# A two-layer streaming trunk on one core: the normalised input built in four-chunk steps on VectorE, and 10 instead of 16 chunks on the unnormalised one

## The chip, the cores and the metric

The kernel runs on one core of a Trainium2 chip. The metric is the device time of one execution in microseconds (us). Engines are named as the profile names them: PE is TensorE's matmuls (PEld its weight loads), DVE is VectorE, ACT is ScalarE, POOL is GpSimd, SP is SyncE, which only issues DMAs here.

## What is computed

A trunk of two layers runs over 304 tokens that share their weights: 16 meta tokens, 256 frames of a new stream and 32 frames of a running one. Activations are kept transposed, channels on the partitions: 1024 channels are eight blocks of 128 x 304. Cut to what matters:

```
def trunk_layer(h, ...):
    h = layer_norm(ALPHA * h + 0.5 * swiglu(h, up1, down1), ln_g[0], ln_b[0])
    q_r, k_r, v_r, g_r, q_s, k_s, v_s, u, gates = split(h @ w_in)
    ...  # retention, stick-breaking attention, pooling, gated merge
    h = layer_norm(ALPHA * h + mix, ln_g[1], ln_b[1])
    h = layer_norm(ALPHA * h + 0.5 * swiglu(h, up2, down2), ln_g[2], ln_b[2])
```

A layer norm takes, for each token, the mean and the variance over all 1024 channels, subtracts, scales, and then applies a gain g and a bias b for each channel. What follows a norm is always a large product: the first feed-forward up-projection, `w_in`, or the second up-projection.

## The kernel before

**Products.** Each product is cut into chunks of 128 output channels. A chunk takes eight weight tiles of 128 x 128, and three matmuls for each tile, since weights and activations are held as a high and a low part (hi x hi, hi x lo, lo x hi): 24 matmuls of 304 columns into one PSUM buffer. Most chunks use a ring of three PSUM buffers (`pd`); a few use a ring of five (`pa`). ACT makes the high part of a weight block (`whi`, `prep_hi`, L234) four chunks ahead, DVE the low part (`wlo`, `prep_lo`, L240) three chunks ahead: one 128 x 1024 instruction on each engine for each chunk. Weights stream from HBM on SP's queue.

**Order.** The order on every engine is the order in which the Python code records instructions; each engine works through its own queue in that order. `dense` (L343) records one chunk. It first lets generators in `side` go one step (`pump`), then runs what was deferred (`tick`), then records the chunk's matmuls with the weight preparation, and lastly lets pending epilogues go one step (`advance`).

**The norm and the unnormalised input.** `Norm` (L429) keeps PE working while the statistics of a norm are still being made. Before the statistics are known, the centred input times the gain, `un` (a high and a low part, `unh` and `unl`), is there. The first `UCHUNKS` = 16 chunks behind a norm multiply this unnormalised input, with two more columns (306 instead of 304) that give for each output channel the product with g and with b. Their results are mended afterwards by `value` (L556): for each such chunk DVE copies the two columns out (`cc`, L559), DVE adds the mean's part (`un<-lnn,cc,pd`, L204), which frees the PSUM buffer, and POOL multiplies by the reciprocal standard deviation (`un<-un,rs_y`). Chunks 0 to 2 are led (their k-parts interleaved) and fill the three `pd` buffers, chunks 3 to 5 use `pa`, chunk 6 takes chunk 0's `pd` buffer again, chunk 9 that of chunk 6, chunk 10 that of chunk 7. From chunk 16 on a chunk multiplies the normalised input `hn` (`hnh`, `hnl`) and has no mending.

`run` (L504) is the norm's own generator. It makes the statistics (`stats`), refines the reciprocal root on DVE (`newton`, which ends with `rs_y<-rs_y,rs_t`), and then, one step for each chunk recorded, makes one of the eight channel blocks of `hn`: POOL adds the negative mean and multiplies (`scale`, L528: `x<-x,lnn`, `x<-x,rs_y`), ACT applies gain and bias (`x<-x,vec`) and makes the high part (`hnh<-x`), DVE the low part (`hnl<-x,hnh`).

**Where it stands.** Five norms work in this way. Three are followed by a feed-forward block (spans begin at about 683, 912 and 1570 us in the profile). There a pair of chunks is a gate and an up half: ACT takes the sigmoid (`sg<-un,cc`), DVE multiplies twice (`sg<-un,cc,sg`, in that order) and makes the low part (`sl<-sg,sh`) of what ACT rounds (`sh<-sg`). For normalised chunks the two multiplications read PSUM (`sg<-sg,pd`) and the low part is POOL's. Two norms are followed by `w_in` (at about 243 and 1143 us). Its first 24 chunks are, twice over, four keys (`ks`), four values (`vs`) and four queries (`qs`), which ACT copies out of `un`. After every second value chunk `v_transposes` (L669) records four PE transposes of the finished `vs`; the first four stand in PE's queue right ahead of chunk 8 and read the values of chunks 4 and 5.

Of the kernel before, what the change touches and what calls it, by code (L numbers as in the profile page):

```python
# [10 lines left out]
F32 = mybir.dt.float32  # L11
F32R = mybir.dt.float32r
AF = mybir.ActivationFunctionType
ALU = mybir.AluOpType

D = 1024
KD = 8
# [6 lines left out]
T = MP + SMP  # L24
# [8 lines left out]
EPS_S = EPS / (ALPHA * ALPHA)  # L33
SCALE = 128.0 ** -0.5
TW = T + 2
UCHUNKS = 16
TPD = 8
NRAW = 5
AHEAD = 3
# [128 lines left out]
def trunk(ctx, tc, xT, wts, kc_d, vc_d, s0_d, sp_d, vec_d, tab_d, y_d, kv_d, ret_d, pool_d):  # L168
# [10 lines left out]
    V, A, G, PE, SP = nc.vector, nc.scalar, nc.gpsimd, nc.tensor, nc.sync  # L179
# [7 lines left out]
    def pair_r(name):  # L187
        return ([newquad(f"{name}h{i}", F32R) for i in range(2)],
                [newquad(f"{name}l{i}", F32R) for i in range(2)])
# [10 lines left out]
    def tt(e, out, a, b, op):  # L200
        e.tensor_tensor(out=out, in0=a, in1=b, op=op)  # L201
# [4 lines left out]
    def act(out, in_, f=AF.Copy, **kw):  # L206
        A.activation(out, in_, f, **kw)  # L207
# [135 lines left out]
    def dense(xs, c0, c1=T, pool=None, nside=2):  # L343
        pump(nside)
        tick()
        ps = pa() if pool == "a" else psd.tile([128, 512], F32, tag="d", name="pd")
        n = len(xs)
        o = ps[:, c0:c1]
        for k, (xh, xl) in enumerate(xs):
            wh, wl = wtile()  # L350
            PE.matmul(o, wh, xh[:, c0:c1], start=(k == 0), stop=False)  # L351
            PE.matmul(o, wh, xl[:, c0:c1], start=False, stop=False)  # L352
            PE.matmul(o, wl, xh[:, c0:c1], start=False, stop=(k == n - 1))  # L353
        advance()
        return ps
# [22 lines left out]
    def hl_list(hl, n):  # L378
        return [(hl[0][k // 4][:, k % 4], hl[1][k // 4][:, k % 4]) for k in range(n)]
# [33 lines left out]
    def split_t(x):  # L413
        n = x.shape[-1]
        hi, lo = t304("st_hi", F32R)[:, 0:n], t304("st_lo", F32R)[:, 0:n]
        split(hi, lo, x)
        return hi, lo


    def mean(i, parts, c):  # L420
        p = pa()
        PE.matmul(p[:, c], onesr[:, i], parts[0], start=True, stop=False)
        PE.matmul(p[:, c], onesr[:, i], parts[1], start=False, stop=True)
        return p
# [4 lines left out]
    class Norm:  # L429
# [19 lines left out]
        def chunk(self, n, ps, scale):  # L449
            c, r = self.c, self.r(n)  # L450
            stt(V, r, ps[:, c], scale, r, ALU.mult, ALU.add)
            if n == 1:
                self.s0 = t304("ln0", F32R)
                tt(G, self.s0[:, c], self.r(0), r, ALU.add)
            elif n == 2:
                p = pa()
                PE.matmul(p[:, c], onesr[:, 0], self.s0[:, c], start=True, stop=True)
                self.piv = t304("lnp")
                act(self.piv[:, c], p[:, c])
            elif n == 3:  # L460
                for i in range(4, KD):
                    tt(G, self.r(i), self.r(i), self.piv[:, c], ALU.subtract)
            for i in {3: (0, 1), 4: (2, 3, 4)}.get(n, (n,) if n > 4 else ()):
                start(self.centre(i))
# [39 lines left out]
        def run(self):  # L504
            c = self.c
            parts = [split_t(x[:, c]) for x in (self.s, self.q)]
            yield
            self.stats(*[mean(1, p, c) for p in parts])
            yield
            self.newton()  # L510
            self.ready = True
            self.hl = pair_r("hn")
            yield
            yield
            for n in range(KD + 2):
                if n < KD:
                    self.scale(n)
                if 1 <= n <= KD:
                    r, gb = self.r(n - 1), self.gb[:, n - 1]
                    act(r, r, AF.Identity, scale=gb[:, 0:1], bias=gb[:, 1:2])  # L520
                    act(self.hl[0][(n - 1) // 4][:, (n - 1) % 4, self.c], r)
                if n >= 2:
                    i, j = (n - 2) // 4, (n - 2) % 4
                    hi, lo = self.hl[0][i][:, j, self.c], self.hl[1][i][:, j, self.c]
                    tt(V, lo, self.r(n - 2), hi.bitcast(F32), ALU.subtract)
                yield

        def scale(self, n):  # L528
            r = self.r(n)
            tt(G, r, r, self.nm[:, self.c], ALU.add)  # L530
            tt(G, r, r, self.rs[:, self.c], ALU.mult)

        def finish(self):
            c = self.c
# [35 lines left out]
        def dense(self, c0, epi):  # L570
            i = self.used
            self.used += 1
            if i >= UCHUNKS:
                ps = dense(hl_list(self.hl, KD), c0)
# [11 lines left out]
            self.pending.append((ps, c0, epi))  # L586
            if i == UCHUNKS - 1:
                while self.gen in side:
                    pump(1)
            k = 0  # L590
            while self.ready and self.pending and (k < 2 or i == UCHUNKS - 1):
                p, o, e = self.pending.pop(0)
# [433 lines left out]
    with tc.manual_schedule():  # L1026
# [10 lines left out]
        for l in range(DEPTH):  # L1037
            last = l == DEPTH - 1
            c0 = META if last else 0
            c = slice(c0, T)  # L1040
# [93 lines left out]
            for g in POOL_GROUPS:  # L1134
                ps2 = [(ph[(2 * g + k) // 4][:, (2 * g + k) % 4], plo[(2 * g + k) // 4][:, (2 * g + k) % 4])
                       for k in range(2)]
                for i in range(2):
                    n = 2 * g + i
                    p = dense(ps2, c0, pool="a" if i else None)
                    s = vec[:, VEC_PS + l * 8 + n:VEC_PS + l * 8 + n + 1]  # L1140
                    hi, lo = oph[n // 4][:, n % 4, c], opl[n // 4][:, n % 4, c]
# [60 lines left out]
```

## Time and profile before

| | |
|---|---|
| time, median of 3 runs | 1796.91 us (1795.27 to 1797.0) |
| the profiled execution | 1797.08 us, its span 1795.3 us |
| PE busy in the span | 1752.5 us (98%), 12704 matmuls |
| DVE, ACT, POOL busy | 1127.6, 846.6 and 536.3 us |
| DMA | 281.19 MB, 157 GB/s on average |
| mean granted clock of TensorE | 0.995 of full speed |

The 1.8 us between the execution's time and its span lie around the program. Busy shares are averages over stages; a start-to-start distance of matmuls tells more than the busy time of PE, whose matmuls overlap.

### The profile page before, as it was taken

Reading aid. Unit: us, or ns where it says so; the run is one execution under the profiler, and the core shown is the slowest. Engines: PE = TensorE matmul, PEld = TensorE weight load, DVE = VectorE, ACT = ScalarE, POOL = GpSimd, SP = SyncE. Lnnn points to the kernel's source line nnn. Section 1 sums busy time; section 2 is a strip of 40 time slices with the busy share of each in tenths; the row PEclk is TensorE's granted clock in tenths of the full one; section 3 lists DMA queues with packets and bytes.
Section 4 is the critical chain, followed back from the end, with each engine's and each line's share of the span. In section 5 each row is a group of like instructions: output and inputs, shape, how many; then the busy total and the mean of one; then the engine's idle time right before and its main releaser. Section 6 shows DMA issues by size and latency. Waiting matters only on the chain.

```text
span 1795.3 us, 31702 instructions
## 1 busy us (share of the span) xinstructions
PE 1752.5 (98%) x12704; PEld 1733.4 (97%) x12704; DVE 1127.6 (63%) x1632; ACT 846.6 (47%) x1354; POOL 536.3 (30%) x546
## 2 busy tenths in 40 slices
PE   8999999999999999999999999999999999989996
PEld 8999999999999999999999999999999899989996
DVE  5444567755685569844588445677566855796444
ACT  5444456444544445544445444574445444554442
POOL 1111345210172245411345113352000622472112
PEclk9999999999999999999999999999999999999998
DMA  7555466344445444545545545663444455445551
GB/s 279 154 159 159 153 204 215 117 145 129 133 119 188 154 141 140 165 155 163 154 129 164 154 155 156 204 211 129 150 133 141 120 190 165 154 129 183 165 164 44
DMA packets 81924, 281.19 MB, mean 157 GB/s; under 512 B 8688, under 2 KB 15728, under 8 KB 81648
## 3 DMA queue, kind: packets, MB, share of 16 engines
q1 hardware_dynamic: 81136, 277.06, 48.6%
q8 instruction: 100, 1.64, 0.4%
q0 software_dynamic: 640, 2.10, 0.3%
q14 instruction: 48, 0.39, 0.1%
HBM read 270.62 MB, written 8.50 MB: 155 GB/s over the span
## 4 chain that ended last, share of the span: by engine, by line
PE 86%; DVE 8%; POOL 2%; issue 1%; DMA 1%; ACT 1%; SPq 0%; ACTq 0%; DVEq 0%; POOLq 0%
PE pd L351 26%; PE pd L352 26%; PE pd L353 26%; DVE wlo L201 3%; DVE sg L204 2%; POOL pw L201 1%; PE pd L371 1%; PE pd L369 1%; PE pd L370 1%; DVE sl L201 1%; PE pa L352 1%; PE pa L351 0%; PE pa L353 0%; PE pa L889 0%; DVE hnl L201 0%
## 5 line engine op out<-in xcount | busy, mean ns | idle before, releaser
L201 DVE TENSOR_TENSOR wlo<-raw,whi 128x1024 fp32r<-128x1024 f32 (+1 forms) x495 | 636.1, 1288 | 179.3 <-PE pd L353 96.2
L207 ACT ACTIVATE whi<-raw 128x1024 fp32r<-128x1024 f32 (+1 forms) x495 | 515.6, 1047 | 178.6 <-PE pd L352 129.0
L351 PE MATMUL pd<-hnh,whi 128*128 128x304 f32 (+1 forms) x1696 | 519.0, 306 | 4.2 <-ACT pu L207 4.2
L352 PE MATMUL pd<-hnl,whi 128*128 128x304 f32 (+1 forms) x1696 | 511.3, 301 | 0.0
L353 PE MATMUL pd<-hnh,wlo 128*128 128x304 f32 (+1 forms) x1696 | 510.9, 301 | 0.0
L351 PEld LDWEIGHTS pd<-hnh,whi 128*128 128x128 f32 x1696 | 321.1, 189 | 5.9 <-ACT pu L207 4.7
L352 PEld LDWEIGHTS pd<-hnl,whi 128*128 128x128 f32 x1696 | 321.6, 190 | 0.7
L353 PEld LDWEIGHTS pd<-hnh,wlo 128*128 128x128 f32 x1696 | 321.1, 189 | 0.0
L352 PE MATMUL pd<-sl,whi 128*128 128x304 f32 (+1 forms) x704 | 212.2, 301 | 0.0
L351 PE MATMUL pd<-sh,whi 128*128 128x304 f32 (+1 forms) x704 | 212.1, 301 | 0.0
L353 PE MATMUL pd<-sh,wlo 128*128 128x304 f32 (+1 forms) x704 | 211.9, 301 | 0.0
L201 DVE TENSOR_TENSOR sg<-sg,pd 128x304 f32<-128x304 f32 (+1 forms) x128 | 59.7, 466 | 195.5 <-ACT sg L207 123.6
L201 POOL TENSOR_TENSOR sl<-sg,sh 128x304 fp32r<-128x304 f32 (+1 forms) x64 | 76.9, 1202 | 343.3 <-ACT sh L207 343.3
L201 POOL TENSOR_TENSOR un<-un,rs_y 128x304 f32<-128x304 f32 (+1 forms) x80 | 95.0, 1195 | 169.4 <-DVE cc L559 122.3
L207 ACT ACTIVATE sh<-sg 128x304 fp32r<-128x304 f32 (+1 forms) x88 | 39.9, 456 | 206.2 <-DVE sg L201 143.7
L351 PE MATMUL pd<-unh,whi 128*128 128x306 f32 (+1 forms) x400 | 122.6, 306 | 12.8 <-DVE un L204 12.8
L353 PEld LDWEIGHTS pd<-sh,wlo 128*128 128x128 f32 x704 | 132.9, 189 | 0.0
L351 PEld LDWEIGHTS pd<-sh,whi 128*128 128x128 f32 x704 | 132.8, 189 | 0.0
L352 PEld LDWEIGHTS pd<-sl,whi 128*128 128x128 f32 x704 | 132.8, 189 | 0.0
L352 PE MATMUL pd<-unl,whi 128*128 128x306 f32 (+1 forms) x400 | 120.7, 302 | 0.0
L353 PE MATMUL pd<-unh,wlo 128*128 128x306 f32 (+1 forms) x400 | 120.7, 302 | 0.0
L353 PE MATMUL pd<-xh,wlo 128*128 128x304 f32 x336 | 102.9, 306 | 0.0
(295 smaller groups left out, 3295.9 us busy)
## 6 DMA issues: line engine op xcount, KB each, us to landing
raw<-in_wts SPq DMA_DIRECT2D x490, 512.0 KB, 3.6
kc<-in_kc SPq DMA_DIRECT2D x8, 512.0 KB, 5.9
vc<-in_vc SPq DMA_DIRECT2D x8, 512.0 KB, 6.4
out_kv<-ks SPq DMA_DIRECT2D x4, 608.0 KB, 5.5
out_kv<-vs SPq DMA_DIRECT2D x4, 608.0 KB, 5.9
out_ret<-st POOLq DMA_DIRECT2D x8, 256.0 KB, 2.3
tab<-in_tab SPq DMA_DIRECT2D x1, 1753.0 KB, 8.9
x<-in_xT SPq DMA_DIRECT2D x4, 304.0 KB, 5.6
```

The lines of the kernel that those rows point to most:

```text
L201: e.tensor_tensor(out=out, in0=a, in1=b, op=op)
L204: e.scalar_tensor_tensor(out=out, in0=a, scalar=s, in1=b, op0=op0, op1=op1)
L207: A.activation(out, in_, f, **kw)
L351: PE.matmul(o, wh, xh[:, c0:c1], start=(k == 0), stop=False)
L352: PE.matmul(o, wh, xl[:, c0:c1], start=False, stop=False)
L353: PE.matmul(o, wl, xh[:, c0:c1], start=False, stop=(k == n - 1))
L369: PE.matmul(o, wh, xh[:, c0:c1], start=(k == 0), stop=False)
L370: PE.matmul(o, wh, xl[:, c0:c1], start=False, stop=False)
L371: PE.matmul(o, wl, xh[:, c0:c1], start=False, stop=(k == len(xs) - 1))
```

## The change

Two things are changed. `UCHUNKS` is 10 instead of 16. And `run` makes `hn` in four steps instead of ten: DVE, not POOL, adds the negative mean and multiplies by the reciprocal deviation, over four channel blocks at once (128 x 4 x 304, the row vectors repeated by a broadcast, `wide`); ACT then does the four blocks' gains, biases and high parts in a row, and DVE the low part of the four at once. The idle step ahead of the first block is dropped, so that the steps stand at chunks 4 to 7.

```
-UCHUNKS = 16
+UCHUNKS = 10
...
-            yield
-            for n in range(KD + 2):
-                if n < KD:
-                    self.scale(n)
-                if 1 <= n <= KD:
-                    r, gb = self.r(n - 1), self.gb[:, n - 1]
-                    act(r, r, AF.Identity, scale=gb[:, 0:1], bias=gb[:, 1:2])
-                    act(self.hl[0][(n - 1) // 4][:, (n - 1) % 4, self.c], r)
-                if n >= 2:
-                    i, j = (n - 2) // 4, (n - 2) % 4
-                    hi, lo = self.hl[0][i][:, j, self.c], self.hl[1][i][:, j, self.c]
-                    tt(V, lo, self.r(n - 2), hi.bitcast(F32), ALU.subtract)
+            for i in range(4):
+                if i < 2:
+                    r = self.h[i][:, :, c]
+                    tt(V, r, r, self.wide(self.nm), ALU.add)
+                    tt(V, r, r, self.wide(self.rs), ALU.mult)
+                if 0 < i < 3:
+                    for j in range(4):
+                        r, gb = self.h[i - 1][:, j, c], self.gb[:, 4 * (i - 1) + j]
+                        act(r, r, AF.Identity, scale=gb[:, 0:1], bias=gb[:, 1:2])
+                        act(self.hl[0][i - 1][:, j, c], r)
+                if i > 1:
+                    hi = self.hl[0][i - 2][:, :, c]
+                    tt(V, self.hl[1][i - 2][:, :, c], self.h[i - 2][:, :, c], hi.bitcast(F32), ALU.subtract)
                 yield
 
-        def scale(self, n):
-            r = self.r(n)
-            tt(G, r, r, self.nm[:, self.c], ALU.add)
-            tt(G, r, r, self.rs[:, self.c], ALU.mult)
+        def wide(self, x):
+            return x[:, self.c].unsqueeze(1).to_broadcast([128, 4, T - self.c0])
```

The order on PE is the same in both but for the operands of chunks 10 to 15. The order on DVE and ACT moves. On DVE, behind the norm of the first layer's second feed-forward block, from the mending of one chunk on (`x_83` and `x_84` are the two halves of the residual, four channel blocks each), before:

```order
L204 SCALAR_TENSOR_TENSOR un<-lnn,cc,pd 128x304
L201 TENSOR_TENSOR wlo<-raw,whi 128x1024
L559 COPY cc<-pd 128x2
L204 SCALAR_TENSOR_TENSOR un<-lnn,cc,pd 128x304
L559 COPY cc<-pa 128x2
L204 SCALAR_TENSOR_TENSOR un<-lnn,cc,pa 128x304
L201 TENSOR_TENSOR wlo<-raw,whi 128x1024
L204 SCALAR_TENSOR_TENSOR sg<-un,cc,sg 128x304 x2
```

The same place on DVE with the change:

```order
L204 SCALAR_TENSOR_TENSOR un<-lnn,cc,pd 128x304
L201 TENSOR_TENSOR x_83<-x_83,lnn 128x4x304
L201 TENSOR_TENSOR x_83<-x_83,rs_y 128x4x304
L201 TENSOR_TENSOR wlo<-raw,whi 128x1024
L560 COPY cc<-pd 128x2
L204 SCALAR_TENSOR_TENSOR un<-lnn,cc,pd 128x304
L560 COPY cc<-pa 128x2
L204 SCALAR_TENSOR_TENSOR un<-lnn,cc,pa 128x304
L201 TENSOR_TENSOR x_84<-x_84,lnn 128x4x304
L201 TENSOR_TENSOR x_84<-x_84,rs_y 128x4x304
L201 TENSOR_TENSOR wlo<-raw,whi 128x1024
L204 SCALAR_TENSOR_TENSOR sg<-un,cc,sg 128x304 x2
```

Four wide instructions have come in between the mendings of chunks 1 and 4; the two wide low parts follow further down, ahead of the weight low parts of chunks 6 and 7.

On ACT, behind the first layer's first norm, ahead of the value copies of chunks 4 and 5 (`vs<-un,cc ... x2`), before:

```order
L207 ACTIVATE ks<-un,cc 128x304 x2
L207 ACTIVATE x_83<-x_83,vec 128x304
L207 ACTIVATE hnh_2543<-x_83 128x304
L207 ACTIVATE whi<-raw 128x1024
L207 ACTIVATE vs<-un,cc 128x304 x2
```

The same place on ACT with the change:

```order
L207 ACTIVATE ks<-un,cc 128x304 x2
L207 ACTIVATE x_84<-x_84,vec 128x304
L207 ACTIVATE hnh_2544<-x_84 128x304
...
L207 ACTIVATE whi<-raw 128x1024
L207 ACTIVATE vs<-un,cc 128x304 x2
```

Where one block's pair of instructions stood, four pairs now stand (the line of dots leaves out three more of the same two rows), those of the second half of the residual; the four pairs of the first half stand further ahead, between the key copies of chunks 0, 1 and those of chunks 2, 3.

## Rows read from the trace of the kernel before

**Rows 1.** The page, part 1: busy us, share of span, instructions.
```profile
PE 1752.5 (98%) x12704; PEld 1733.4 (97%) x12704; DVE 1127.6 (63%) x1632; ACT 846.6 (47%) x1354; POOL 536.3 (30%) x546
```

**Rows 2.** Waits of PE: waiter, releaser, us in total, times, longest.
```profile
PE pd L351 <- DVE un L204: 12.8, 18, 1.0
```

**Rows 3.** Windows, feed-forward blocks: length; busy (instructions) of PE, PEld, DVE, ACT, POOL.
```profile
683.35:703.85 20.50, 20.50 (x146) 20.50 (x145) 18.40 (x31) 11.06 (x18) 12.99 (x12) 1.00 0.40 139
703.85:733.12 29.27, 25.28 (x170) 23.91 (x169) 28.92 (x41) 16.39 (x28) 21.38 (x19) 1.00 0.36 111
912.44:932.76 20.32, 20.32 (x147) 20.32 (x145) 18.16 (x31) 10.88 (x18) 12.74 (x12) 1.00 0.36 113
932.76:962.21 29.45, 25.16 (x171) 23.85 (x169) 29.10 (x41) 16.63 (x29) 21.55 (x19) 1.00 0.37 110
1569.82:1589.28 19.46, 19.46 (x146) 19.46 (x145) 17.43 (x31) 10.46 (x17) 12.13 (x12) 1.00 0.46 158
1589.28:1617.88 28.60, 24.06 (x171) 22.82 (x169) 28.25 (x41) 16.50 (x29) 20.86 (x19) 1.00 0.38 112
```

**Rows 4.** Timeline of PE, first feed-forward norm: start, duration, instruction, idle before.
```profile
708.00 0.38 PE L351 MATMUL pd<-unh,whi 128*128 128x306 f32 x1 [0.57 <-DVE un L204]
```

**Rows 5.** Timeline of DVE, the same block.
```profile
687.50 1.22 DVE L201 TENSOR_TENSOR wlo<-raw,whi 128x1024 fp32r<-128x1024 f32 x1
688.64 0.15 DVE L559 COPY cc<-pd 128x2 f32<-128x2 f32 x1
...
689.91 1.45 DVE L201 TENSOR_TENSOR wlo<-raw,whi 128x1024 fp32r<-128x1024 f32 x1
...
702.64 1.87 DVE L201 TENSOR_TENSOR wlo<-raw,whi 128x1024 fp32r<-128x1024 f32 x1
...
706.68 0.53 DVE L204 SCALAR_TENSOR_TENSOR sg<-un,cc,sg 128x304 f32<-128x304 f32 x1
...
707.32 0.53 DVE L204 SCALAR_TENSOR_TENSOR un<-lnn,cc,pd 128x304 f32<-128x304 f32 x1
```

**Rows 6.** Timeline of POOL, the same block.
```profile
702.48 0.94 POOL L201 TENSOR_TENSOR un<-un,rs_y 128x304 f32<-128x304 f32 x1 [1.11 <-DVE un L204]
```

**Rows 7.** Timeline of DVE, the retention's norm, with POOL idle.
```profile
487.65 0.80 DVE L201 TENSOR_TENSOR rst<-rsy 128x608 f32<-128x608 f32 x1 [0.29 <-ACT rsy L207]
488.48 0.79 DVE L204 SCALAR_TENSOR_TENSOR rst<-var,rst 128x608 f32<-128x608 f32 x1
489.31 0.48 DVE L392 TENSOR_SCALAR rst<-rst 128x608 f32<-128x608 f32 x1
...
492.88 0.47 DVE L201 TENSOR_TENSOR od<-od,rsy 128x304 f32<-128x304 f32 x1
```

**Rows 8.** Timeline of DVE, first layer's w_in.
```profile
247.22 1.22 DVE L201 TENSOR_TENSOR wlo<-raw,whi 128x1024 fp32r<-128x1024 f32 x1
...
249.62 1.45 DVE L201 TENSOR_TENSOR wlo<-raw,whi 128x1024 fp32r<-128x1024 f32 x1
```

**Rows 9.** Timeline of ACT, first layer's w_in.
```profile
257.05 0.64 ACT L207 ACTIVATE x<-x,vec 128x304 f32<-128x304 f32 x1 [2.04 <-POOL x L201]
257.73 0.46 ACT L207 ACTIVATE hnh<-x 128x304 fp32r<-128x304 f32 x1
258.09 1.05 ACT L207 ACTIVATE whi<-raw 128x1024 fp32r<-128x1024 f32 x1
259.04 0.97 ACT L207 ACTIVATE vs<-un,cc 128x304 f32<-128x304 f32 x2
```

**Rows 10.** Timeline of PE, first layer's w_in.
```profile
259.92 0.60 PE L673 MATMUL pa<-tab,vs 128*128 128x128 f32 x4
260.27 0.39 PE L351 MATMUL pd<-unh,whi 128*128 128x306 f32 x1
```

**Rows 11.** Windows around PE's longest stop; the seventh figure is the granted clock.
```profile
525.80:529.20 3.40, 0.26 (x2) 0.01 (x1) 1.42 (x5) 0.44 (x3) 3.24 (x10) 1.00 0.50 154
529.20:532.60 3.40, 3.30 (x13) 3.31 (x14) 2.63 (x3) 2.16 (x6) 3.23 (x8) 0.50 0.00 0
```

**Rows 12.** Timeline of PE just behind that stop.
```profile
529.30 0.62 PE L351 MATMUL pd<-hnh,whi 128*128 128x304 f32 x1 [3.24 <-ACT pu L207]
529.72 0.46 PE L352 MATMUL pd<-hnl,whi 128*128 128x304 f32 x1
529.97 0.46 PE L353 MATMUL pd<-hnh,wlo 128*128 128x304 f32 x1
```

## The prediction

> **What bounds the kernel now.** The page comes first: PE is busy 98% of the span, DVE 63%, ACT 47%, POOL 30% [rows 1]. So a change on DVE, ACT and POOL moves the time only where PE waits for them. The waits of PE name one such place that this change touches: 18 times a matmul on the unnormalised input waited for DVE's `un`, the step that frees a PSUM buffer [rows 2]. They lie in the three feed-forward blocks, six in each. Their true cost is read from the windows, because PE's idle time counts only what is left when the pipeline has drained. Chunks 3 to 8 of the first block, six chunks, take 20.50 us, 3.42 each; at that rate chunks 9 to 15, seven chunks, would take 23.9, and they take 29.27: 5.35 us lost. In the second block it is 29.45 against 23.7, in the third 28.60 against 22.7: 5.75 and 5.9 [rows 3]. Together **17.0 us** are lost, the most that this change could win back there. DVE is busy 28.9 of those 29.3 us [rows 3]: it is the engine that is behind. In the two `w_in` stretches PE loses nothing to the norm, but one thing there is just in time: the four transposes of values ahead of chunk 8 start at 259.92, while ACT's copies of the values of chunks 4 and 5 start at 259.04 and take 0.97, to 260.01 [rows 9, 10]. There is no slack.
>
> **What goes away.** For each norm six chunks lose their two columns and their mending. Two of 306 columns are 0.02 us of a 3.42 us chunk; 30 chunks, 0.6 us gained. POOL's sixteen blocks of `x<-x` and six `un` for each norm go; POOL is not the bound, and what this is worth is only that DVE waits for it less often.
>
> **What comes, and its price.** The trace has no DVE instruction of 4 x 304 elements with a repeated operand. Nearest rows with POOL idle: `TENSOR_TENSOR` of 304 elements 0.47, of 608 elements 0.80 [rows 7], so 0.33 for each further block and 1.45 for four, an estimate. A following instruction starts 0.08 before the end of one that it does not depend on (687.50, 1.22 long, next at 688.64 [rows 5]): 1.36 from start to start. If the wide form ran like `TENSOR_SCALAR`, 0.48 for 608 [rows 7], it would be about 0.8; that is the lower bound. I take 1.45, since it is the same operation.
>
> DVE and POOL hold each other up. A `wlo` is 1.22 free, but 1.87 at 702.64, when POOL had begun its `un` at 702.48 (0.94 long) [rows 5, 6]; at 689.91 it is 1.45, with POOL's first `un` part done [rows 5]. So a DVE instruction that finds POOL at work waits 0.23 to 0.65. I take 0.23 behind the mending of two chunks, and 0.5 to 0.6 for the next one, when POOL's second `un` has gone ahead.
>
> The Trainium skill, "SBUF — State Buffer", section "SBUF: two separate sides", says that the pair of ports which DVE and GpSimd share is an exclusive lock, held by whoever starts first for the whole instruction. The trace agrees that one waits and does not just run slower, but the wait at 702.64 was 0.65, less than the 0.78 that POOL's instruction still had to go. By the rule taken literally each wait would be up to a whole POOL instruction; that case is among the rivals.
>
> **The feed-forward blocks, step by step.** I walk DVE's queue of the first block with the change, from 687.50, where the first `wlo` behind `newton` starts [rows 5]. `wlo` 1.14; mending of chunks 0 and 1, 1.27 (688.64 to 689.91 [rows 5]): 689.9. First wide add 0.23 + 1.45, wide product 0.5 + 1.36: 693.45. `wlo` 1.14, mending of 2 and 3, 1.27: 695.9. Second pair of wide steps, again 3.55: 699.4. `wlo` 1.14; two gate products of 0.53, the second dependent, 1.1 together (706.68 [rows 5]); mending of 4 and 5, 1.27: 702.9. Wide low part 0.2 + 1.36; `wlo` behind POOL's `un`, 0.6 + 1.14; `sl` 0.4 (as 304 elements); two products 1.1; mending of chunk 6, 0.7 to its end: **708.4**. PE starts 0.15 behind that (un at 707.32 + 0.53, matmul at 708.00 [rows 4, 5]): chunk 9 at 708.6, not 703.85, **4.75 us late**. To the mending of chunk 7 it is another wide low part 1.36, `wlo` 1.74, `sl` 0.4, products 1.1, mending 0.63, in all 5.2; chunk 9 itself takes 3.42: **1.8 us** more. To chunk 8's mending it is 3.2, less than a chunk, and from there DVE gets ahead, since normalised chunks have one product each and no mending. So some **6.6 us** are lost in place of 5.35. The loss is not taken away, it comes earlier and in two pieces. The other two blocks stand alike: 6.6 against 5.75 and 5.9. Sum 19.8 - 17.0 = **+2.8 us**. Bounds: without any wait for POOL 2.3 + 0.6 us less, 3.7 lost in each block; with a full 0.65 at every one of POOL's `un` and PE's clock lowered by the stop (below), 10.3. That is -5.9 to +13.9 for the three.
>
> **The w_in stretches.** Here DVE's mendings are early enough, and ACT's queue decides. With the change ACT has four pairs (`x`, `hnh`) between the key copies 0, 1 and 2, 3, and four more ahead of the value copies 4, 5; ahead of each group there is a wait for DVE's wide product, and PE's transposes stand ahead of chunk 8 as before. DVE: 249.62 (the second `wlo` of before [rows 8], now the first wide add) + 0.23 + 1.45 + 0.5 + 1.45 = 253.25. ACT from there: a pair is 1.04 (257.05 to 258.09 [rows 9]), four are 4.15; a `whi` 0.95 (258.09 to 259.04 [rows 9]); two copies 0.9; four pairs 4.15 (the second half's product is done on DVE at 253.2 + 1.14 + 1.27 + 3.6 = 259.2, just then); `whi` 0.95; two value copies 1.0: 265.35. The four transposes follow in half a microsecond with their end hidden, chunk 8 starts near 265.7, not 260.27 [rows 10]: **5.4 us**. What is late next: the mending of chunk 6, at about 265.7, is needed 3.4 later, so nothing. Queued behind ACT's waits are `whi` of the chunks ahead, which have four chunks of lead. Bounds of the stop: 4.7 without a wait for POOL, 6.8 if POOL's `un` for chunks 2 and 3 are held up by the wide product and ACT waits on them too.
>
> A stop of that length has a second price. PE's longest stop now, the 3.24 us ahead of 529.30 [rows 12], ends with the granted clock at 0.5, that is 1.2 in place of 2.4 GHz, for 3.4 us [rows 11]. Matmuls then start 0.25 apart [rows 12], against 0.14 (146 in 20.50 us [rows 3]); 13 of them [rows 11] cost 13 x 0.11 = 1.5 us. I take 1.5 for each stretch, with bounds 0 (the clock doesn't fall) and 3 (it stays low twice as long). In the feed-forward blocks a lowered clock would be hidden by the wait of chunk 10. Sum for two stretches 2 x (5.4 + 1.5) = **+13.8 us**, between 9.4 and 19.6.
>
> **Sum.** +13.8 + 2.8 - 0.6 = +16.0. The profiled execution took 1797.08 (its span and 1.8 around it), so 1813.1; it lies 0.2 above the median of the runs, so 1812.9, **1813 us**, 0.9% slower.
>
> **Rivals.** (a) *DVE gets through in time*, the faster side: the wide form runs at 0.8 and meets no POOL instruction. Five wide steps of 0.65 less and 2.3 us of waits less bring the mending of chunk 6 from 708.4 to 702.9, ahead of 703.85, which is the point from which it decides: then all 17.0 us of the feed-forward blocks come back, the first half on ACT starts 2 us earlier, and `w_in` loses some 4 us in each stretch with no fall of the clock: 1797 - 17.0 - 0.6 + 8 = 1787. Against it speaks the 0.80 of a 608-element `TENSOR_TENSOR`. (b) *About even*: only one of these two holds. Then the blocks win 6 to 9 us and `w_in` loses 9 to 11 with the clock: 1797 to 1801. (c) *POOL holds for its whole instruction*, as the lock rule reads: six waits of about 0.85 (`un` 0.94, just begun) in place of 2.3 us in all, 2.8 us more in each block and about 1 us more in each `w_in` stretch: 1813 + 8.4 + 2 = 1823. (d) *The stop is longer than I read, or the clock stays low in all five places*: each block at its upper bound, 1826 and more, to 1830.
>
> **How the numbers follow.** The forecast has 0.66, (a) 0.07, (b) 0.07, (c) 0.12, (d) 0.08. The forecast's own bounds, not all reached together, are 1801 to 1824; with (c) the range is 1801 to 1826, and (a), part of (b) and (d) are left out. A measurement of this kernel tells 0.2%, 3.6 us, from no change. Slower by more than that: 0.66 + 0.12 + 0.08 = 0.86; (b) is mostly within it, 0.07; (a) is faster, 0.07.
>
> **What would show it.** On PE in the profile of the changed kernel: a stop of about 5 us ahead of the four transposes before chunk 8 behind the first and the fourth norm, with the granted clock at 0.5 behind it, and the transposes' releaser ACT's `vs`; in each feed-forward block two waits on `un` at chunks 9 and 10, some 6.6 us together, and none at chunks 11 to 15. On DVE the wide steps at 1.4 to 2.1 us. The forecast is wrong if ACT's value copies are done by 260 although eight pairs stand ahead of them, or if the wide steps take under 1 us.

## The result, and the profile after

The changed kernel takes **1813.22 us** (median of 4 runs, 1812.95 to 1814.89), the kernel before 1796.09 (1794.87 to 1797.0): a ratio of 1.0095, 95% interval 1.0082 to 1.0108. The forecast was 1813.0. The profiled execution took 1814.89 us, its span 1813.1, at a mean granted clock of 0.988 (0.995 before). All three engines that feed PE have less to do than in [rows 1], and PE is busy for longer. The page, part 1:

```profile
PE 1759.5 (97%) x12704; PEld 1742.0 (96%) x12704; DVE 1098.5 (61%) x1553; ACT 845.8 (47%) x1354; POOL 436.0 (24%) x445
```

The waits of PE (waiter, releaser, us in total, times, longest):

```profile
PE pd L351 <- DVE un L204: 14.2, 5, 4.6
PE pa L674 <- ACT vs L207: 9.6, 2, 4.8
```

In [rows 2] 18 short waits for `un` made up 12.8 us, none over 1.0. Now there are five, and three long ones, 4.5 to 4.6 us each, are nearly all of the 14.2. The second row is new: the four transposes (L674 in this kernel) wait for ACT's copies of the values, once behind the first norm and once behind the fourth.

PE's order hardly differs between the two kernels, so the distance from the first matmul of chunk 3 to the first matmul of chunk 22 can be compared, in us:

| stretch behind a norm | before | after | difference | forecast |
|---|---|---|---|---|
| first `w_in` | 71.74 | 78.90 | +7.16 | +6.9 |
| first feed-forward block | 70.11 | 72.29 | +2.18 | +1.25 |
| second feed-forward block | 70.26 | 71.29 | +1.03 | +0.85 |
| second `w_in` | 70.71 | 77.68 | +6.97 | +6.9 |
| third feed-forward block | 67.51 | 67.97 | +0.46 | +0.7 |
| sum | | | +17.80 | +16.6 |

The two profiled executions differ by 1814.89 - 1797.08 = 17.81 us, so outside these five stretches nothing is left, but only as a sum. From the first `w_in` to the first feed-forward block the changed kernel takes 1.55 us longer: the granted clock is at 0.5 there for 6.8 us from 536.3 on, before for 3.4 us from 529.2 on. From the second `w_in` to the third block it takes 1.59 less: before, the clock is at 0.5 for 3.4 us from 1430.3 on, after not at all. That the clock is the reason of these two differences was not tested. The profiled execution also lies 1.7 above the median of its kernel.

**w_in.** PE in the first one (start, duration, instruction, idle before), then ACT, DVE and POOL:

```profile
265.31 1.13 PE L674 MATMUL pa<-tab,vs 128*128 128x128 f32 x4 [4.81 <-ACT vs L207]
266.10 0.60 PE L351 MATMUL pd<-unh,whi 128*128 128x306 f32 x1
266.50 0.46 PE L352 MATMUL pd<-unl,whi 128*128 128x306 f32 x1
266.75 0.46 PE L353 MATMUL pd<-unh,wlo 128*128 128x306 f32 x1
```
```profile
258.78 0.97 ACT L207 ACTIVATE ks<-un,cc 128x304 f32<-128x304 f32 x2
259.69 0.64 ACT L207 ACTIVATE x<-x,vec 128x304 f32<-128x304 f32 x1
...
263.42 0.46 ACT L207 ACTIVATE hnh<-x 128x304 fp32r<-128x304 f32 x1
263.78 1.04 ACT L207 ACTIVATE whi<-raw 128x1024 fp32r<-128x1024 f32 x1
264.73 0.97 ACT L207 ACTIVATE vs<-un,cc 128x304 f32<-128x304 f32 x2
```
```profile
250.06 1.65 DVE L201 TENSOR_TENSOR x<-x,lnn 128x1216 f32<-128x1216 f32 x1
251.74 1.94 DVE L201 TENSOR_TENSOR x<-x,rs_y 128x1216 f32<-128x1216 f32 x1
...
257.69 1.96 DVE L201 TENSOR_TENSOR x<-x,rs_y 128x1216 f32<-128x1216 f32 x1
```
```profile
249.58 2.82 POOL L201 TENSOR_TENSOR un<-un,rs_y 128x304 f32<-128x304 f32 x2 [30.87 <-DVE cc L560]
...
261.56 2.80 POOL L201 TENSOR_TENSOR un<-un,rs_y 128x304 f32<-128x304 f32 x2 [3.20 <-DVE cc L560]
```

Between the key copies (258.78) and the value copies (264.73) ACT works without a pause, on four pairs and a `whi`. PE has nothing to do for 4.81 us; its transposes start behind the first copy, the third of them waits for the second copy, and chunk 8 starts at 266.10. POOL's rows are used further down: its two products of chunks 0 and 1 last until 252.40, and the `un` of chunk 5 is done at 264.36, not much ahead of ACT's copy of it.

The granted clock around that stop, in windows of PE (length; PE's busy time and instructions, granted clock, DMA share, GB/s):

```profile
263.20:266.60 3.40, 1.29 (x6) 0.50 0.17 60
266.60:270.00 3.40, 3.40 (x15) 0.50 0.42 145
270.00:273.40 3.40, 3.40 (x26) 0.99 0.88 265
```

At 0.50 (1.2 GHz) 15 matmuls start in 3.40 us, at 0.99 (2.4 GHz) 26. Chunk 8 takes 5.24 us, in the kernel before 3.47.

**The feed-forward blocks.** The windows that answer to [rows 3], chunks 3 to 8 and 9 to 15 of the first two blocks:

```profile
692.49:717.87 25.38, 20.74 (x147) 20.26 (x145) 23.21 (x35) 16.79 (x29) 8.48 (x7) 0.99 0.33 103
717.87:744.42 26.55, 26.55 (x168) 26.55 (x169) 22.26 (x31) 12.82 (x20) 9.81 (x6) 0.88 0.55 171
924.33:949.78 25.45, 20.78 (x147) 20.32 (x145) 23.21 (x35) 16.84 (x29) 8.48 (x7) 0.99 0.28 79
949.78:975.34 25.56, 25.28 (x168) 25.07 (x169) 22.11 (x31) 12.82 (x20) 9.76 (x6) 0.94 0.59 176
```

The first part is 4.9 to 5.1 us longer than in [rows 3], the second 2.7 to 3.9 shorter. The loss has moved ahead: it is now one long stop before chunk 9, with a low clock behind it. The rows of DVE up to that stop, the counterpart of [rows 5], and PE's first matmul behind it:

```profile
712.13 1.72 DVE L201 TENSOR_TENSOR hnl<-x,hnh 128x1216 fp32r<-128x1216 f32 x1
713.77 1.85 DVE L201 TENSOR_TENSOR wlo<-raw,whi 128x1024 fp32r<-128x1024 f32 x1
715.54 0.46 DVE L201 TENSOR_TENSOR sl<-sg,sh 128x304 fp32r<-128x304 f32 x1
715.93 1.16 DVE L204 SCALAR_TENSOR_TENSOR sg<-un,cc,sg 128x304 f32<-128x304 f32 x2
...
717.19 0.53 DVE L204 SCALAR_TENSOR_TENSOR un<-lnn,cc,pd 128x304 f32<-128x304 f32 x1
717.64 1.42 DVE L201 TENSOR_TENSOR hnl<-x,hnh 128x1216 fp32r<-128x1216 f32 x1
...
722.41 0.53 DVE L204 SCALAR_TENSOR_TENSOR un<-lnn,cc,pd 128x304 f32<-128x304 f32 x1
```
```profile
717.87 0.59 PE L351 MATMUL pd<-unh,whi 128*128 128x306 f32 x1 [4.59 <-DVE un L204]
```

### The profile page after: what moved, and what is told of

Read it like the earlier page. It is cut to its first block, busy times and chain, and to the rows that moved or that the text cites. A ratio compares the mean times of both kernels' runs of the same rounds, so it can differ in the third digit from the quotient of the medians.

```text
span 1813.1 us, 31505 instructions
## 1 busy us (share of the span) xinstructions
PE 1759.5 (97%) x12704; PEld 1742.0 (96%) x12704; DVE 1098.5 (61%) x1553; ACT 845.8 (47%) x1354; POOL 436.0 (24%) x445
## 4 chain that ended last, share of the span: by engine, by line
PE 87%; DVE 7%; ACT 2%; POOL 2%; issue 2%; DMA 1%; SPq 0%; ACTq 0%; DVEq 0%; POOLq 0%
PE pd L351 26%; PE pd L352 26%; PE pd L353 26%; DVE wlo L201 2%; DVE x L201 1%; PE pd L370 1%; POOL pw L201 1%; PE pd L371 1%; PE pd L369 1%; DVE un L204 1%; ACT x L207 1%; PE pa L890 0%; DVE sg L204 0%; DVE hnl L201 0%; PE pa L894 0%
## 5 line engine op out<-in xcount | busy, mean ns | idle before, releaser
L351 PE MATMUL pd<-hnh,whi 128*128 128x304 f32 (+1 forms) x1936 | 591.6, 306 | 4.6 <-ACT pu L207 4.0
L352 PE MATMUL pd<-hnl,whi 128*128 128x304 f32 (+1 forms) x1936 | 584.3, 302 | 0.0
L353 PE MATMUL pd<-hnh,wlo 128*128 128x304 f32 (+1 forms) x1936 | 583.2, 301 | 0.0
L351 PEld LDWEIGHTS pd<-hnh,whi 128*128 128x128 f32 x1936 | 367.2, 190 | 6.3 <-ACT pu L207 4.5
L352 PEld LDWEIGHTS pd<-hnl,whi 128*128 128x128 f32 x1936 | 366.5, 189 | 0.7
L353 PEld LDWEIGHTS pd<-hnh,wlo 128*128 128x128 f32 x1936 | 366.5, 189 | 0.0
L201 POOL TENSOR_TENSOR un<-un,rs_y 128x304 f32<-128x304 f32 (+1 forms) x50 | 76.5, 1543 | 196.7 <-DVE cc L560 157.0
L351 PE MATMUL pd<-xh,whi 128*128 128x304 f32 x336 | 102.4, 305 | 0.0
L352 PE MATMUL pd<-xl,whi 128*128 128x304 f32 x336 | 101.3, 301 | 0.0
L207 ACT ACTIVATE sg<-pd 128x304 f32<-128x304 f32 (+1 forms) x89 | 37.4, 420 | 123.8 <-PE pd L353 123.8
```

## The experiments

The theory that the result left standing: in `w_in` PE waits for the eight pairs on ACT, in the feed-forward blocks for DVE's wide steps, and behind long stops it runs for a while at half the clock. The rivals were the number of chunks, GpSimd, and the place of the steps. All runs in one table; the distances are those of the table above.

| run | median us | ratio to before, 95% | w_in 1, 2 | feed-forward 1, 2, 3 |
|---|---|---|---|---|
| before | 1796.1 | | 71.74, 70.71 | 70.11, 70.26, 67.51 |
| after | 1813.22 | 1.0082 to 1.0108 | 78.90, 77.68 | 72.29, 71.29, 67.97 |
| e1, wide steps, 16 chunks | 1814.45 | 1.0088 to 1.0118 | 78.55, 78.27 | 71.43, 71.33, 69.31 |
| e2, 10 chunks, old steps | 1839.91 | 1.0229 to 1.0263 | 80.82, 79.39 | 79.07, 79.62, 76.50 |
| e3, pairs spread | 1816.81 | 1.0105 to 1.0135 | 78.56, 76.76 | 74.10, 72.59, 69.34 |
| e4, without wide adds, products | 1791.69 | 0.9968 to 0.9989 | 77.01, 77.01 | 65.37, 65.18, 62.25 |
| e5, all spread, 16 chunks | 1796.52 | 0.999 to 1.0009 | 71.71, 70.43 | 69.90, 70.15, 67.40 |
| e6, as e5, two chunks later | 1796.73 | 0.9996 to 1.0015 | 71.70, 70.85 | 69.79, 69.87, 69.13 |
| e7, after, PE kept at work | 1811.97 | 1.0074 to 1.0104 | 77.02, 75.85 | 72.18, 71.21, 67.98 |
| e8, after, product on DVE | 1816.25 | 1.0096 to 1.0126 | 78.81, 79.17 | 72.56, 72.38, 68.29 |
| e9, e5 with product on DVE | 1798.05 | 1.0 to 1.0019 | 71.71, 70.42 | 70.11, 70.05, 69.28 |
| e10, e9 with `cc` on ACT | 1812.94 | 1.0077 to 1.0107 | 73.20, 71.95 | 75.38, 75.39, 72.87 |
| e11, e9 with 12 chunks | 1807.25 | 1.0045 to 1.0075 | 72.62, 71.93 | 73.55, 73.64, 71.80 |
| e13, e5, a low part earlier | 1789.83 | 0.9952 to 0.9979 | 71.71, 70.44 | 68.60, 68.87, 66.17 |

### The two halves of the change alone (e1, e2)

e1 is the changed kernel with the old number:

```
-UCHUNKS = 10
+UCHUNKS = 16
```

> The wide steps alone: the changed kernel with UCHUNKS back at 16. Theory (queues): what costs time is where the wide steps and the eight ScalarE pairs stand in the queues, not how many chunks are mended. The two w_in stretches lose the same 7 us each (stop of 5.4 ahead of the transposes, clock 1.8), the feed-forward blocks again lose 6.6 to 7.9 us at chunks 9 and 10, and no more behind that, since with GpSimd free a pair of mended chunks costs VectorE about 6.2 us against 6.8 on PE: 1811 to 1816 us. Rival (ten chunks are too few): the normalised input is wanted too early, so 16 chunks bring the time back to 1796 to 1800, or below it by the relief of GpSimd.

Measured 1814.45, in the theory's range. Six more mended chunks in each block made no difference that can be measured (1813.66 to 1815.91 against 1812.95 to 1814.89): the stops are those of the changed kernel, but for the third block's, which is 0.4 longer, and chunks 10 to 15 run at 3.2 to 3.5 us each. Waits of PE in e1:

```profile
PE pd L351 <- DVE un L204: 14.2, 4, 4.9
PE pa L674 <- ACT vs L207: 9.6, 2, 4.8
```

e2 is the kernel before with `UCHUNKS = 10` and nothing else.

> The other part alone: the kernel before with UCHUNKS 10, block by block on GpSimd. Ten steps of the norm's generator don't fit in front of chunk 10, so the last ones are recorded in a burst behind chunk 9, and GpSimd has some 12 operations of 1.0 to 1.2 us left then. Theory: chunk 10 waits for the normalised blocks one after another, about 12 us in each feed-forward block, of which 3.4 come back since the later waits for PSUM buffers are gone, and about 5 us in each w_in stretch: 1797 + 3 x 9 + 2 x 5 = 1834, between 1820 and 1850. Rival: the GpSimd steps catch up in time and the mending saved counts, 1785 to 1797.

Measured 1839.91, in the theory's range. Without the wide steps ten chunks are far too few: GpSimd's blocks come one for each chunk, and chunk 10 waits for the normalised input, block after block. It takes 16.1 us in the first two feed-forward blocks and 11 in `w_in`, in place of 3.4, partly at a granted clock of 0.5. Waits of PE in e2:

```profile
PE pd L352 <- DVE hnl L201: 23.0, 21, 3.3
PE pd L351 <- ACT hnh L207: 4.5, 6, 1.3
```

So the number alone costs 44 us, the wide steps at their early place 18, and both together 17. The wide steps make the input early enough for ten chunks; that ten chunks suffice gains nothing.

### Which engine makes the stops (e3, e4)

e3 leaves DVE's wide adds and products where they are and records two pairs with each chunk from chunk 5 on (the low parts at chunks 7 and 9):

```
-            for i in range(4):
+            for i in range(6):
...
-                if 0 < i < 3:
-                    for j in range(4):
-                        r, gb = self.h[i - 1][:, j, c], self.gb[:, 4 * (i - 1) + j]
+                if 0 < i < 5:
+                    for n in (2 * i - 2, 2 * i - 1):
+                        r, gb = self.r(n), self.gb[:, n]
```

> The changed kernel with ScalarE's eight pairs spread, two for each chunk from chunk 5 on, and VectorE's two wide low parts at chunks 7 and 9. ScalarE then has four pairs fewer ahead of the value copies of chunks 4 and 5. Theory A (ScalarE's queue alone made the stop): the copies come about 4 us earlier, the stop ahead of chunk 8 shrinks from 5.4 to about 1.2 us and the clock does not fall, 12 us less: about 1801. Theory B (both queues are late: GpSimd's result for chunk 5, held up by VectorE's wide steps, came at 264.4 in the changed kernel, 0.8 before the copy that reads it): the stop shrinks by about 1 us only, to 4.2 to 4.6, the clock still falls, and the feed-forward blocks gain about 1 us each since a wide low part goes behind chunk 9's release: 1807 to 1812.

Measured 1816.81; both theories missed it. The stop in `w_in` shrank by 1.0 us only: chunk 7 with its stop takes 8.17 in place of 9.13. ACT in e3, ahead of the transposes:

```profile
261.50 0.55 ACT L207 ACTIVATE vs<-un,cc 128x304 f32<-128x304 f32 x1 [0.48 <-POOL un L201]
263.26 0.55 ACT L207 ACTIVATE vs<-un,cc 128x304 f32<-128x304 f32 x1 [1.22 <-POOL un L201]
```

ACT is idle now. It waits for POOL's `un`, which waits for DVE's wide steps. In the feed-forward blocks the stop before chunk 9 became 1.3 us shorter, since one low part has left its way, but chunk 10 now waits for that low part. Waits of PE in e3:

```profile
PE pd L351 <- DVE un L204: 11.4, 5, 3.2
PE pa L675 <- ACT vs L207: 7.3, 4, 2.5
PE pd L352 <- DVE hnl L201: 7.3, 3, 2.4
```

e4 is the changed kernel without the four wide adds and products of each norm; the normalised input is then not normalised.

```
-                if i < 2:
-                    r = self.h[i][:, :, c]
-                    tt(V, r, r, self.wide(self.nm), ALU.add)
-                    tt(V, r, r, self.wide(self.rs), ALU.mult)
```

> The changed kernel without the four wide VectorE steps that add the mean and multiply by the deviation (they are left out; the wide low parts and ScalarE's pairs stay). VectorE's queue is then some 7 us shorter ahead of chunk 6's mending. Theory (both queues): in the feed-forward blocks chunk 6 is mended in time, and the 17 us that the kernel before loses there are gone; in w_in ScalarE still does eight pairs ahead of the value copies of chunks 4 and 5, which end near 264.6, so the stop is still 4 to 4.7 us, and the clock falls: 1797 - 17.6 + 12 = 1792, between 1787 and 1796. Rival (VectorE's wide steps are the whole cause): the stop in w_in is gone too, about 1779.

Measured 1791.69, as the theory had it. The feed-forward blocks are 5.7 to 6.9 us shorter than in the changed kernel; some 1 us of loss is left in each, at chunk 9. The stop in `w_in` stays, at 3.72 of idle time instead of 4.81:

```profile
263.57 1.13 PE L670 MATMUL pa<-tab,vs 128*128 128x128 f32 x4 [3.72 <-ACT vs L207]
```

The pair of runs shows two chains in `w_in` that end within a microsecond of each other: ACT's eight pairs, and DVE's wide steps with POOL's `un` behind them. Taking either away alone wins 1 us of the 5.4; e5, below, spreads both, and the stop is gone. In the feed-forward blocks it is DVE.

### The price of the clock (e7)

```
+        if warm:
+            for k in range(40):
+                PE.matmul(p[:, 0:256], onesr[:, 0], onesr.rearrange("p a b -> p (a b)"), start=True, stop=True)
```

These matmuls stand in `v_transposes`, in front of the first transposes of each `w_in`, and go into the tile that the transposes then write.

> The changed kernel with 40 matmuls of 256 columns on constants, whose result the transposes overwrite, ahead of the transposes before chunk 8 of the two w_in stretches: TensorE works through most of its stop of 5 us there. Theory (the stop costs its own length and, because the granted clock falls in it, 1.5 to 1.8 us more behind it): the clock stays at 1.0 behind the stop and 3 to 3.6 us go, 1809.7 (1808.5 to 1811). Rival (the chunks behind the stop are slow for another reason, such as weights or mendings that are late too): 1812 to 1814, with chunk 8 as long as before.

The same columns over the place where the clock had been low, in e7:

```profile
263.00:266.40 3.40, 3.35 (x26) 1.00 0.20 67
266.40:269.80 3.40, 3.40 (x26) 1.00 0.40 143
```

The clock stays at 1.00, and chunk 8 takes 3.46 and 3.32 in place of 5.24 and 5.00. That is 1.78 + 1.68 = 3.5 us, in the traces 3.7 for the two stretches with what the transposes win. The median fell by 1.25 only, to 1811.97, above the expected 1808.5 to 1811; the profiled executions differ by 2.9. The profiled run of the changed kernel lies 1.7 above its own median, so the traces show the place and the price there, and the medians can't confirm the full size.

### GpSimd (e8, e9)

e8 is the changed kernel with the mending's product on the other engine:

```
-            tt(G, t[:, c], t[:, c], self.rs[:, c], ALU.mult)
+            tt(V, t[:, c], t[:, c], self.rs[:, c], ALU.mult)
```

> The changed kernel with the product of the mending (un by rs_y) on VectorE in place of GpSimd. Theory (GpSimd's instruction holds VectorE up by 0.2 to 0.65 us each, as the prediction's sum has it): seven mendings cost VectorE 0.45 each, 3.2, and save it some 2.3 us of waits ahead of chunk 9, so a feed-forward block gets 0.9 us worse; a w_in stretch wins about 0.6: 1814.7 (1812 to 1817). Rival (GpSimd holds the ports for a whole instruction each time): 5 us of waits go, a block wins 2 us, a w_in stretch 1.5: 1804 (1802 to 1807).

Measured 1816.25, within the theory's range. With POOL out of the way the wide steps run at their own length:

```profile
250.02 1.42 DVE L201 TENSOR_TENSOR x<-x,lnn 128x1216 f32<-128x1216 f32 x1
251.47 1.43 DVE L201 TENSOR_TENSOR x<-x,rs_y 128x1216 f32<-128x1216 f32 x1
```

So POOL had cost the first one 0.23 (1.65) and the second one 0.5 (1.94). Chunk 9 starts 0.4 to 0.5 us later in each block, since the products on DVE cost more than these waits. The stop ahead of it is no longer than before (4.5 us); what is new is a wait of 0.5 to 0.7 for `wlo` inside chunk 8. In `w_in` the expected gain of 0.6 was a loss of 0.6 and 0.85 in the stop. A product costs DVE more than the expectation had it: from the start of `un` to the wide add it is 0.96 (249.06 to 250.02) instead of 0.45, so 0.51. Four of them stand ahead of the second half's wide product, 2.0, and the four waits removed give 1.5 back. The rival, 10 us faster, is out.

e9 makes the same edit in the spread version e5 (below).

> The spread version with 16 chunks, and the product of the mending (un by rs_y) on VectorE instead of GpSimd. Theory (in the steady state of the spread version each GpSimd product holds the next VectorE instruction with two SBUF operands up by about 0.65, seen as 1.12 for 0.46, 1.88 for 1.22): the product on VectorE costs 0.39 from start to start, so each mended chunk from chunk 6 on gets 0.26 shorter on VectorE, 2 to 3.5 us for a feed-forward block: 1787 (1784 to 1791). Rival (the waits are as small as those of the changed kernel's first mendings, 0.22 and 0.52, where the same edit cost 0.4 a block): 1796 to 1799.

Measured 1798.05 (1795.30 to 1801.07; the profiled run is the fastest of the ten), the rival. In e5 POOL's products hold later DVE instructions up by 0.65 in the steady state, and yet the blocks are no shorter with the product on DVE (the third is 1.9 longer). A product at 0.51 against a wait of 0.65 there, and of 0.23 to 0.5 for the first chunks, leaves little to win; this sum is a reading of the traces, not a test.

### Taking the groups apart (e5, e6, e10, e11, e13)

e5 records at most one wide step of DVE and one pair of ACT with a chunk. The steps of `run` become a table, one entry for each chunk from chunk 5 on; `add`, `mul`, `pair` and `lo` are the instructions of the changed kernel:

```
-UCHUNKS = 10
+UCHUNKS = 16
...
+            yield
+            for step in ((('add', 0),), (('mul', 0),), (('pair', 0),), (('pair', 1), ('add', 1)), (('pair', 2),), (('pair', 3), ('mul', 1)), (('pair', 4), ('lo', 0)), (('pair', 5),), (('pair', 6),), (('pair', 7),), (('lo', 1),)):
```

> The changed kernel with 16 chunks on the unnormalised input and the work of the norm taken apart: behind one chunk each, a wide add or product on VectorE (chunks 5, 6, 8, 10), one block's pair on ACT (chunks 7 to 14), the wide low parts at chunks 11 and 15. No group of pairs stands ahead of the value copies, so both theories have no stop in the w_in stretches: 14 us less than the changed kernel. Theory A (the sum of VectorE's work decides): with 16 mended chunks VectorE has no idle time to take up the wide steps (busy 98 to 99% in chunks 10 to 15 of the run with 16 chunks), so each feed-forward block still loses 4 to 6 us, only at later chunks: 1796 to 1801. Theory B (the place decides, the wide steps stood where the mendings were most behind): a block loses 1 to 2 us, 1785 to 1790.

Measured 1796.52, the kernel before to within 0.1%. The `w_in` stretches are those of the kernel before. The feed-forward blocks lose what they lost before, in more and smaller waits. Waits of PE in e5:

```profile
PE pd L351 <- DVE un L204: 8.3, 15, 1.0
PE pd L352 <- DVE hnl L201: 5.3, 3, 1.9
```

e6 starts the same work two chunks later and packs it somewhat closer, with DVE's first wide step behind the mending of chunk 6 (16 chunks, in spite of its label).

> As the spread version, with all of VectorE's wide steps behind the mending of chunk 6 (the first add at chunk 7, the last product at chunk 10) and the 16 chunks kept. Chunk 9 then waits for nothing wide. Theory A (the sum decides): the loss moves from chunk 9 to chunks 10 to 15 and is as large as in the spread version, within 2 us of its time, 1796 to 1801. Theory B (the place decides): the earliest mendings come in time and the later ones too, 1783 to 1789.

Measured 1796.73. Chunks 8 and 9 of the first two blocks lose nothing now, chunks 11 and 12 lose more. Both runs came out as theory A had it: moving all of the work to another place wins nothing, which fits a loss that follows the sum of DVE's work.

e10 lets ACT copy the two columns, `act(cc, ps[:, T:TW])` in place of `V.tensor_copy`, on top of e9.

> As the run before in this list, and the copies of the two columns (cc) on ScalarE. Theory (VectorE's work per mended chunk is what the feed-forward blocks wait for): 0.19 less for each mended chunk, 2 to 2.5 us for a block: 6 to 7 us less than the run without it, about 1780. Rival (the copies stand behind ScalarE's sigmoids and weight parts and come late, so the mending waits for them): the same as the run without it, or up to 5 us more.

Measured 1812.94, 15 us slower, three times what the rival allowed. DVE and ACT in e10:

```profile
706.56 0.53 DVE L204 SCALAR_TENSOR_TENSOR un<-lnn,cc,pd 128x304 f32<-128x304 f32 x1 [1.02 <-ACT cc L207]
```
```profile
705.58 0.46 ACT L207 ACTIVATE sh<-sg 128x304 fp32r<-128x304 f32 x1 [4.92 <-DVE sg L204]
705.94 0.53 ACT L207 ACTIVATE sg<-un,cc 128x304 f32<-128x304 f32 x1
706.38 0.15 ACT L207 ACTIVATE cc<-pd 128x2 f32<-128x2 f32 x1
```

ACT's copy of 0.15 stands behind a rounding that waits for DVE's last product. DVE then waits for the copy, 1.02 here and 1.02 again at the next mending. Two queues that had run side by side became one chain.

e11 is e9 with 12 chunks, and the steps closer together.

> As the first run of this list (product on VectorE), with 12 instead of 16 chunks on the unnormalised input and the wide steps and pairs closer together, so that the normalised input is there at chunk 12. Theory (up to the chunk where the normalised input is needed VectorE's work for a mended chunk lasts about as long as TensorE's chunk, so that their number decides nothing): within 3 us of the run with 16. Rival (each mended chunk costs something, four fewer in a block win 2 to 4 us there): 6 to 12 us faster than the run with 16.

Measured 1807.25, slower than both expected. The chunk that first needs the normalised input, chunk 12, takes 6.7 to 7.5 us, and PE waits 1.4 us for `un` ahead of chunk 10, which it doesn't in e9. Fewer mended chunks spare DVE some work, but the rest has to be done sooner. Number and spacing were changed together here, so neither has a price of its own.

e13 changes one thing in e5: the second low part is recorded at chunk 14, not 15, and the pairs 6 and 7 ahead of it one chunk earlier too.

```
-... (('pair', 5),), (('pair', 6),), (('pair', 7),), (('lo', 1),)):
+... (('pair', 5), ('pair', 6)), (('pair', 7),), (('lo', 1),)):
```

> The spread version with 16 chunks, the second wide low part one chunk earlier (chunk 14, its pairs 5 and 6 both at chunk 12). In the spread version chunk 16 of a feed-forward block waits 1.9 us for that low part, which stands on VectorE behind the mending of chunk 14, and that mending is needed only by chunk 17. Theory (only the order on VectorE keeps the low part late, and what moves behind it has slack): 1.3 to 1.9 us less for each block, 4 to 5.5 together, about 1792 (1790.5 to 1794), which would be faster than both kernels. Rival (VectorE is a whole stretch behind, so the wait moves to chunks 17 and 18): within 1 us of the spread version, 1795.5 to 1797.5.

Measured **1789.83** (1789.16 to 1790.87), ratio 0.9965, interval 0.9952 to 0.9979: faster than both kernels, and a little under the range expected. Waits of PE in e13:

```profile
PE pd L351 <- DVE un L204: 9.9, 18, 1.0
```

The wait for `hnl` is gone, and little has come in its place: chunk 16 of the three blocks takes 4.0 instead of 5.3, chunk 17 at most 0.1 more. That is 1.2 to 1.3 a block, 3.8 together, just under the 4 to 5.5 of the theory. The medians differ by 6.7, and the rest is not the blocks': the profiled runs differ by 5.4, of which 1.5 lie between the second `w_in` and the third block, where the granted clock falls at 1428.9 in e5 and not in e13 (e13 has a fall at 529.4 that e5 has not, at no visible cost). The last 1.3 are the scatter of e5 (1793.28 to 1797.86), whose profiled run lies 1.6 below its median. Against the kernel before the three blocks are 4.2 shorter, of 6.4 between the medians. So the order on DVE is shown for some 4 us; the range of the total was missed for reasons that were not settled. What this adds to theory A: the sum of the work is as it was, but a piece that is needed first had stood behind one that is needed a chunk later.

## Why the prediction was right

**The w_in stop, forecast 5.4.** Measured from chunk 7's start, chunk 8 starts 9.13 and 9.10 later, before 3.73 and 3.75: 5.40 and 5.35. The walk was right also in its parts. The stretch begins 0.43 later in the trace of after; with that, the walk has the first half's product done at 253.68, the value copies at 265.78, chunk 8 at 266.1. The trace has 253.69, 265.70, 266.10. **The clock, forecast 1.5:** chunk 8 is 1.77 and 1.71 longer, and e7 shows that it is the clock. The term was a little low: the clock is at 0.50 from 263.2 to 270.0, 4.7 us of which lie behind the stop, and some 16 matmuls run in them, not 13.

**"What is late next: ... nothing"** was too short a look. The mending of chunk 6 was indeed no matter. But POOL's `un` of chunk 5 ends at 264.36, 0.4 before the copies begin. The sum didn't depend on it; a repair does, as e3 found out.

**The feed-forward blocks, forecast +2.8, measured +3.7.** The trace has the block 9.14 later (chunk 3 at 692.49, [rows 3] 683.35). With that shift the walk's points up to the mending of chunks 4 and 5 are within 0.1 us of the trace, and its mending of chunk 6 ends at 717.54, the trace says 717.72. Chunk 9 was forecast for 717.74 and starts at 717.87. The mending of chunk 7 follows 5.2 later by the walk, 722.41 - 717.19 = 5.22 in the trace. What failed is a smaller sentence: "In the feed-forward blocks a lowered clock would be hidden by the wait of chunk 10". The clock did fall in all three blocks. In the second and third chunk 9 takes 5.22 and 5.05, no more than DVE's mending of chunk 7 needs; hidden, as forecast. In the first the clock stayed low for 6.8 us, not 3.4, and chunk 9 took 6.22: 1.0 us shows. For the same reason the two waits on `un` at chunks 9 and 10 are one wait of 4.6 us and one slow chunk.

**The wide step, taken as 1.45,** is 1.42 alone and 1.65 to 1.96 beside POOL (e8 and the rows of after), so the waits of 0.23 and 0.5 to 0.6 were right too. **The two columns, -0.6:** chunks of the first block that the mending doesn't hold up take 3.39 in the changed kernel and 3.41 in e1, 0.02 a chunk as forecast; too little to be measured by itself.

**The rivals.** (a) needed wide steps of 0.8 and no POOL in their way, (b) one of the two; the 0.80 of [rows 7] was the right neighbour, not the 0.48. (c) would have had waits of 0.85. The Trainium skill, "SBUF — State Buffer", section "SBUF: two separate sides", has one engine hold the shared ports for its whole instruction. The traces agree that one engine waits until the other is done: POOL's `un`, 0.84 alone, makes 2.82 for two when the second meets a wide step. In length the two nearly meet. When DVE's wide product starts at 251.74, POOL has 0.66 to go, to 252.40, and the product is 0.52 longer than its 1.42. POOL's product at 717.87 takes 1.89, to 719.76; the `wlo` that starts at 718.98 has 0.78 of it ahead and takes 1.86, 0.64 more than 1.22. In all 66 `wlo` (128 x 1024) and wide steps (128 x 1216) of after's trace that met a POOL instruction, DVE waited for what that instruction had left by the profile, less 0.13 to 0.14 us. So (c) did not fail on the rule: it took every POOL instruction as just begun, and DVE's steps found 0.36 to 0.78 left. The six waits ahead of chunk 9 come to 2.5 us, forecast 2.3, by (c) 5.1. (d) named the right event, the clock falling in all five places, and the wrong price, since three of the falls lie beside a wait that is there anyway.

The sum without the columns was 16.6, the traces have 17.8: 0.9 more in the first block, mostly the clock, 0.2 in the second, 0.3 in `w_in`, 0.2 less in the third block. The medians differ by 17.1. That 1813.22 lies 0.2 from the forecast is in part luck: by the medians the sum with the columns, 16.0, was 1.1 too small, and the time that it was added to, 1796.9, lay 0.8 above the 1796.09 of the kernel before in the result. The mechanism, the places and the sizes of the two main terms don't depend on that.

## What to carry to other kernels

A group of instructions that is handed to an in-order engine in one piece delays everything that is queued behind it, however idle that engine is on average: ACT is busy 47%, and eight pairs ahead of two copies still stop PE for 3.7 us when DVE's wide steps are left out (e4). Before such a stop is repaired, look for the second chain that ends at nearly the same time, since removing one alone wins only the difference. Where one engine is behind for a whole stretch, moving its work about as a whole won nothing here (e5, e6); what can still be won is to let each piece stand in the order in which its result is needed, as e13 did with one low part.

## What was not expected of the hardware

DVE and POOL stop each other in both directions, and the longer step does the greater harm: POOL's product takes 0.84 alone and 2.0 behind a wide DVE step, DVE's steps at most 0.66 more behind POOL. Not every DVE step is held up. In after's trace those that read two tiles of SBUF are, while the mending's `un`, which reads PSUM, never takes longer than 0.53 (min, median and longest in ns, of 35):

```profile
L204 DVE SCALAR_TENSOR_TENSOR un<-lnn,cc,pd x35: 512/530/532, 249.0 to 1622.3; 128x304 f32<-128x304 f32 x26, 128x288 f32<-128x288 f32 x9
```

That PSUM is the reason was not tried. The clock fell at each of the five long stops of after and stayed at 0.50 for 3.4 us at two of them and 6.8 at three; matmuls on constants kept it up. The 3.24 us stop of [rows 12] ended with a low clock, the same stop in e5, 3.24 too, did not. What decides was not found.
